# Output projection with two of its four column blocks by seven half products, the sums of weights formed by adding DMAs

## The chip, the cores and the metric

The kernel runs on one core of one Trainium2 chip. The metric is the device time of one execution in microseconds (us); lower is better. The kernel before takes 1097.7 us, the median of 3 runs (1097.32 to 1098.1).

## The reference

One layer of a hybrid decoder trunk on 512 tokens of width 2048, all in float32. With h = RMSNorm(x), the program computes

```python
z = h @ W_in                       # columns: r, k, v, two small loras | gate | pool input | pool gate
...                                # token shift, decay, rate
S_t = S_{t-1} (diag(w_t) - kk_t^T (a_t * kk_t)) + v_t^T k_t        # 16 heads of 64
y_t = S_t r_t                      # then a norm per head and a bonus
y_pool = pooled means @ w_pool * pool_scale
y_mix = concat(y_rwkv * silu(gate), y_pool * silu(pool gate))
x = x + y_mix @ W_out
x = x + sigmoid(x @ W_pg + b_pg) * (p @ W_ple)
return rms_norm(x, final_g)
```

The change is about `y_mix @ W_out`: 512 x 2048 times 2048 x 2048.

## The kernel before, in words

Every large product is made of three TensorE matmuls: each operand is split into a rounded part (hi) and a rest (lo), and `mm3` (L157) issues hi·hi, lo·hi and hi·lo into one PSUM bank. A tile of weights is 128 x 512 (256 KB). `wsplit` (L127 to L134) loads it on SyncE's (SP's) queue, casts it on ACT (`whi`, L132) and subtracts on DVE (`wlo`, L133); the weight tiles have four buffers. `split` (L136 to L139) does the same for activations (L137 on ACT, L138 on DVE).

The program runs in this order. First x is loaded, normed and transposed into `hhi`, `hlo`. Then the columns of z are produced one block after the other. Their matmuls come from a stream (`pump`) that fills TensorE between the steps of the recurrence, in the order of the program: TensorE's instructions stand in a pinned order there (`pin[0]`, `keep_in_program_order`), so a matmul that waits holds all that follow. The eight pairs of heads are prepared one after the other: `prepare_key`, `decay_and_rate`, `norm_key`, `scale_key`, `prepare`, `scores`, `invert`, `gather`, and then `recur` runs the recurrence in eight chunks of 64 tokens. Of a pair, the steps of which the prediction speaks are these:

- `decay_and_rate` casts the small weights of the loras on ACT (`us`, `uaz`, `as`: L524, L525) and multiplies by them (`pu`, `pa`); `norm_key` squares the keys into `kqh` and sums them by a matmul (`pss`). The loads of the small weights go over ACT's own DMA queue (L354).
- `invert` works on DVE, with one copy on POOL (`xw<-i`, L660).
- `recur` updates the state per chunk: a product `ps` on TensorE, then on DVE `sbd` = `ps` times a column of `pw` plus `s0p` (L807, L809), where `s0p` is the old state with its decay, formed on POOL (L816).

The output projection (`proj` with "o", L940) comes after the last recurrence. `y_mix` returns from DRAM in sixteen tiles of 128 x 512 (`load_y`, `yin`, L918) and is split into `yhi`, `ylo`. Each of four blocks of 512 columns takes 16 tiles of weights (in the order `order`), and per tile 4 groups of 128 tokens with 3 matmuls each: 192 matmuls of 512 columns a block, 768 in all. After each block DVE adds the residual (L995), ACT's queue stores the sum (`x2d`), and `turn` transposes it on TensorE (L1002) and splits it (`x2hi`, `x2lo`) for the gate's projection `acc_g`, which follows.

The tile scheduler orders the instructions of each engine; outside the pinned part they may stand in another order than the code.

Of the kernel before, what the change touches and what calls it, by code (L numbers as in the profile page):

```python
# [28 lines left out]
O_U, O_GP = O_G + DR, O_G + 2 * DR  # L29
KAPPA = math.exp(-0.5)  # L30
CK = 4


@with_exitstack
def trunk_kernel(ctx: ExitStack, tc: tile.TileContext, x, p, norm_g, w_in, mu, w0, w_up, a0, a_up,
# [84 lines left out]
    def dp(o, i):  # L120
        return dprm[:, o + i:o + i + 1]

    hhi = hp.tile([P, KT, T], F32R, name="hhi", tag="ahi")
    hlo = hp.tile([P, KT, T], F32R, name="hlo", tag="alo")


    def wsplit(src, kt, n, nm):  # L127
# [277 lines left out]
    def pool_unit(n):  # L405
        g, i = n // 4, n % 2
        win = WINDOWS[g]
        ps = psA.tile([P, T], F32, name=f"zb{n}", tag="acc")
        yield from zcols(ps, f"b{n}")
        if n % 4 < 2:  # L410
            u_ = pp.tile([P, T], F32, name=f"u{n}", tag="u")
            nc.scalar.copy(u_, ps)
            s_ = u_
            w_ = 1
            while w_ < win:
                n_ = pp.tile([P, T], F32, name=f"sw{n}_{w_}", tag="sw")
# [21 lines left out]
        nc.scalar.dma_start(out=yd[NJ + m], in_=sgp)  # L438

    phl, pn = [], []  # L440

# [314 lines left out]
    def recur(j, work, between):  # L756
# [17 lines left out]
        for ch in range(NCH):  # L774
            par, q = ch % 2, ch // 2
            pb = 64 * (1 - par)
            cur, nxt = sbd[ch % 2], sbd[(ch + 1) % 2]
            pcc = pw[:, ch, C:C + 1]
            sl = slice((ch % 4) * P, (ch % 4 + 1) * P)
            if ch % 4 == 0:  # L780
                py = psY.tile([P, T], F32, name=f"py{j}_{ch}", tag="y")
            zs = zsp[par]
            if ch > 0:
                mm(py[:, sl], ar[:, q, 2 * par:2 * par + 2, :], cur, start=ch in (1, 4), stop=True,
                                 skip_group_check=True)
# [12 lines left out]
            step()  # L798
            pump(HC2)
            if ch < NCH - 1:  # L800
                pss = psS.tile([P, T], F32, name=f"ps{j}_{ch}", tag="s")
                mm(pss[:, 0:P], bkn[:, ch, :], uv[:, ch, :], start=True, stop=True)
                for h in range(2):
                    hc = slice(64 * h, 64 * h + 64)
                    with tc.high_priority(offset=HP):
                        if ch == 0:
                            lead[0] = nc.vector.tensor_scalar(nxt[hc, hc], pss[hc, hc], pcc[hc], None, ALU.mult)  # L807
                        else:
                            lead[0] = nc.vector.scalar_tensor_tensor(nxt[hc, hc], pss[hc, hc], pcc[hc], s0p[hc, :],  # L809
                                                                     ALU.mult, ALU.add)  # L810
                s0p = rw.tile([P, C], F32, name=f"s0p{j}_{ch}", tag="s0p", bufs=2)
                pcn = pw[:, ch + 1, C:C + 1]
                if ch < NCH - 2:
                    for h in range(2):
                        hc = slice(64 * h, 64 * h + 64)
                        nc.gpsimd.tensor_scalar(s0p[hc, :], nxt[hc, hc], pcn[hc], None, ALU.mult)  # L816
# [62 lines left out]
    scale_key(0)  # L879
    prepare(0)  # L880
    pump(H3)
    scores(0)
    pump(H2)
    for _ in invert(0):
        pass
    pump(HT)
# [25 lines left out]
    yhi = ymp.tile([P, KT, T], F32R, name="yhi")  # L912
    ylo = ymp.tile([P, KT, T], F32R, name="ylo")
    AHEAD = 6

    def load_y(k):
        t_ = ymp.tile([P, T], F32, name=f"yin{k}", tag="yin", bufs=AHEAD)
        nc.scalar.dma_start(out=t_, in_=yd[k])  # L918
        split(yhi[:, k, :], ylo[:, k, :], t_)

    for k in order[:AHEAD]:
        load_y(k)
# [1 line left out]
    pin[0] = False  # L924


    x2hi = hp.tile([P, KT, T], F32R, name="x2hi", tag="ahi")
    x2lo = hp.tile([P, KT, T], F32R, name="x2lo", tag="alo")
    x2d = dram.tile([T, D], F32, name="x2d", bufs=1)

    KEEP, LATE = 8, 4
# [8 lines left out]
    def proj(w, hi_, lo_, ec, nm, ks=range(KT), tts=range(NT), keep=None, aside=None):  # L940
        acc = {tt: acc_tile(f"acc_{nm}{ec}_{tt}") for tt in tts}
        for i, k in enumerate(ks):
# [9 lines left out]
            else:  # L952
# [11 lines left out]
                keep[k] = (wh, wl)  # L964
                if i >= LATE:
                    continue
            for tt in tts if keep is None or i >= LATE else tts[:-1]:
                ts_ = slice(tt * P, (tt + 1) * P)
                first = i == (LATE if keep is not None and tt == NT - 1 else 0)
# [14 lines left out]
            nc.scalar.dma_start(out=t_, in_=pled[tt * P:(tt + 1) * P, ec * EC:(ec + 1) * EC])  # L984
            ples[ec].append(t_)

    for ec in range(D // EC):
        es = slice(ec * EC, (ec + 1) * EC)
        acc = proj(w_out, yhi, ylo, ec, "o", order)
        x2 = []  # L990
        for tt in range(NT):
            rows = slice(tt * P, (tt + 1) * P)
            t_ = pp.tile([P, EC], F32, name=f"x2_{ec}_{tt}", tag=("u", "sw")[tt // 2])
            nc.scalar.dma_start(out=t_, in_=x[rows, es])
            nc.vector.tensor_tensor(t_, acc[tt], t_, ALU.add)  # L995
            nc.scalar.dma_start(out=x2d[rows, es], in_=t_)
            x2.append(t_)
        def turn(ec=ec, x2=x2):
            for i in range(EC // P):
                pt = psM.tile([P, T], F32, name=f"px2_{ec}_{i}", tag="m")  # L1000
                for tt in range(NT):
                    nc.tensor.transpose(pt[:, tt * P:(tt + 1) * P], x2[tt][:, i * P:(i + 1) * P], ident)  # L1002
                hi = split(x2hi[:, 4 * ec + i, :], x2lo[:, 4 * ec + i, :], pt)
            return hi


        if ec < D // EC - 1:
            turn()

    sy.close()  # L1010

# [1 line left out]
    with tc.tile_pool(name="fp", bufs=2) as fp, tc.tile_pool(name="kp_", bufs=1) as kp_:  # L1013
# [92 lines left out]
        for ec in range(LAST):  # L1106
            pre = {}
            vec = vectors(ec)
            acc = proj(w_pg, x2hi, x2lo, ec, "g", aside=turn if ec == 0 else None)
# [71 lines left out]
```

## Time and profile before

| | |
|---|---|
| median of 3 runs | 1097.7 us (1097.32 to 1098.1) |
| the profiled execution | 1097.72 us |
| its span in the profile | 1095.9 us |
| TensorE (PE) busy | 1070.8 us, 98% |
| VectorE (DVE) busy | 708.2 us, 65% |
| ScalarE (ACT) busy | 448.3 us, 41% |
| GpSimd (POOL) busy | 76.9 us, 7% |
| read from and written to HBM | 118.02 MB, 18.87 MB |

The profiled execution lies at the median; 1.8 us of it are outside the span. Times in the profile are microseconds from the start of the span. Rows of the timeline give the start, the duration, the engine, the line, the operation with its operands (out<-in) and, in brackets, the idle time before it with what ended it. A busy PE is counted from overlapping records (one matmul of 512 columns is recorded with 0.39 us while the next starts 0.23 us later), so the rate is read from starts and not from durations. "ACTq" and "SPq" are the sequencers that issue DMAs.

### The profile page before, as it was taken

What the parts mean: (1) busy time and instruction counts of PE and PEld (TensorE: products, weight loads), DVE (VectorE), ACT (ScalarE), POOL (GpSimd) and SP (SyncE); (2) the same over time, 40 slices, a digit from 0 to 9 for tenths busy, and PEclk for the clock granted to TensorE, in tenths of its full rate; (3) what the DMA queues carried; (4) which work ended last, traced back from release to release, by engine and by line L of the source; (5) the groups of instructions that cost most, each with busy time, mean ns of one, the idle gap of its engine ahead of it and who ended that gap; (6) DMA issues with size and microseconds to landing.
All of it is one profiled execution on the core that took longest, in us unless ns stands there. A gap on an engine that the chain in (4) does not pass through costs nothing.

```text
span 1095.9 us, 17196 instructions
## 1 busy us (share of the span) xinstructions
PE 1070.8 (98%) x6060; PEld 877.6 (80%) x6060; DVE 708.2 (65%) x1835; ACT 448.3 (41%) x917; POOL 76.9 (7%) x180
## 2 busy tenths in 40 slices
PE   5999999999999999999999999999999999999996
PEld 4888878887788888788878788888888888888885
DVE  6687867878688679678886956454433424445366
ACT  7633535345335335353343344543222222233337
POOL 2100110110110110100101101000000000000000
PEclk9999999999999999999999999999999999999999
DMA  7433433332423333333334242775534438455534
GB/s 233 116 96 97 111 92 84 96 100 73 120 82 105 104 92 89 96 82 93 91 94 119 79 138 93 232 233 169 172 124 136 167 99 244 137 189 137 181 106 154
DMA packets 178486, 138.56 MB, mean 126 GB/s; under 512 B 34678, under 2 KB 139743, under 8 KB 178399
## 3 DMA queue, kind: packets, MB, share of 16 engines
q1 hardware_dynamic: 157694, 103.89, 32.1%
q10 hardware_dynamic: 20704, 33.56, 9.8%
q8 instruction: 48, 0.79, 0.3%
q14 instruction: 40, 0.32, 0.1%
HBM read 118.02 MB, written 18.87 MB: 125 GB/s over the span
## 4 chain that ended last, share of the span: by engine, by line
PE 86%; DVE 5%; DMA 4%; ACT 3%; issue 1%; SPq 0%; ACTq 0%; DVEq 0%
PE acc_o L157 16%; PE zb L157 14%; PE acc_g L157 14%; PE zv L157 8%; PE zk L157 7%; PE zg L157 7%; PE zr L157 7%; PE py L157 2%; PE pple L157 2%; PE pm L157 1%; PE pu L157 1%; DMA n<-nd 1%; PE pp L157 1%; DMA raw_g<-in_w_pg_dram 1%; PE ps L157 1%
## 5 line engine op out<-in xcount | busy, mean ns | idle before, releaser
L133 DVE TENSOR_TENSOR wlo_g<-raw_g,whi_g 128x512 fp32r<-128x512 f32 x84 | 57.0, 685 | 79.6 <-ACT whi_g L132 76.5
L157 PE MATMUL zb<-hhi,whi_b 128*128 128x512 f32 x256 | 107.0, 418 | 0.0
L133 DVE TENSOR_TENSOR wlo_o<-raw_o,whi_o 128x512 fp32r<-128x512 f32 x64 | 43.9, 690 | 91.4 <-ACT whi_o L132 91.4
L157 PE MATMUL zb<-hhi,wlo_b 128*128 128x512 f32 x256 | 100.5, 393 | 0.0
L157 PE MATMUL acc_o<-whi_o,ylo 128*128 128x512 f32 x256 | 100.2, 391 | 0.0
L157 PE MATMUL acc_o<-whi_o,yhi 128*128 128x512 f32 x256 | 99.9, 390 | 0.0
L157 PE MATMUL zb<-hlo,whi_b 128*128 128x512 f32 x256 | 99.9, 390 | 0.0
L157 PE MATMUL acc_o<-wlo_o,yhi 128*128 128x512 f32 x256 | 99.8, 390 | 0.0
L132 ACT CAST whi_g<-raw_g 128x512 fp32r<-128x512 f32 x84 | 51.9, 620 | 102.7 <-PE acc_g L157 55.4
L157 PE MATMUL acc_g<-whi_g,x2hi 128*128 128x512 f32 x208 | 81.3, 391 | 0.0
L157 PE MATMUL acc_g<-wlo_g,x2hi 128*128 128x512 f32 x208 | 80.9, 389 | 0.0
L157 PE MATMUL acc_g<-whi_g,x2lo 128*128 128x512 f32 x208 | 80.7, 389 | 0.0
L132 ACT CAST whi_o<-raw_o 128x512 fp32r<-128x512 f32 x64 | 39.9, 623 | 97.0 <-PE acc_o L157 96.7
L816 POOL TENSOR_SCALAR s0p<-sbd,pw 64x64 f32<-64x64 f32 x96 | 56.6, 589 | 322.8 <-DVE sbd L809 255.0
L132 ACT CAST whi_b<-raw_b 128x512 fp32r<-128x512 f32 x64 | 39.7, 621 | 86.5 <-PE zv L157 35.4
L133 DVE TENSOR_TENSOR wlo_b<-raw_b,whi_b 128x512 fp32r<-128x512 f32 x64 | 43.8, 685 | 34.2 <-ACT whi_b L132 32.9
L157 PEld LDWEIGHTS zb<-hhi,wlo_b 128*128 128x128 f32 x256 | 48.0, 188 | 11.1
L661 DVE TENSOR_TENSOR xw<-xw,tm 128x60 f32<-128x60 f32 (+24 forms) x248 | 52.1, 210 | 6.8
L157 PEld LDWEIGHTS acc_o<-wlo_o,yhi 128*128 128x128 f32 x256 | 48.1, 188 | 10.3 <-DVE wlo_o L133 0.4
L157 PEld LDWEIGHTS acc_o<-whi_o,yhi 128*128 128x128 f32 x256 | 48.1, 188 | 9.7
L157 PEld LDWEIGHTS acc_o<-whi_o,ylo 128*128 128x128 f32 x256 | 48.1, 188 | 9.8
L157 PEld LDWEIGHTS zb<-hhi,whi_b 128*128 128x128 f32 x256 | 48.2, 188 | 8.5
(285 smaller groups left out, 2550.0 us busy)
## 6 DMA issues: line engine op xcount, KB each, us to landing
raw_b<-in_w_in_dram SPq DMA_DIRECT2D x64, 256.0 KB
raw_o<-in_w_out_dram SPq DMA_DIRECT2D x64, 256.0 KB
raw_g<-in_w_pg_dram SPq DMA_DIRECT2D x64, 256.0 KB
raw_k<-in_w_in_dram SPq DMA_DIRECT2D x32, 256.0 KB
raw_r<-in_w_in_dram SPq DMA_DIRECT2D x32, 256.0 KB
raw_v<-in_w_in_dram SPq DMA_DIRECT2D x32, 256.0 KB
raw_g<-in_w_in_dram SPq DMA_DIRECT2D x32, 256.0 KB
n<-nd SPq DMA_DIRECT2D x16, 256.0 KB
```

The costliest lines, as they stand in the source:

```text
L132: nc.scalar.copy(hi, raw)
L133: nc.vector.tensor_tensor(lo, raw, hi.bitcast(F32), ALU.subtract)
L157: i = nc.tensor.matmul(*a, **k)
L661: nc.vector.tensor_tensor(xw[:, 0:n_, s + 1:32], xw[:, 0:n_, s + 1:32], tm[:, 0:n_, 0:w_], ALU.add)
L816: nc.gpsimd.tensor_scalar(s0p[hc, :], nxt[hc, hc], pcn[hc], None, ALU.mult)
```

## The change

Blocks 1 and 2 of the four column blocks are computed together by a seven-product scheme on halves: the rows of W_out are paired (tile 2q with tile 2q + 1), the tokens are cut into two halves, and in place of eight products of halves there are seven, on sums of halves. Each product takes 8 tiles of weights, and per tile 2 groups of 128 tokens with 3 matmuls: 7 x 8 x 2 x 3 = 336 matmuls for the two blocks, where there were 384. Four of the seven take sums of activations (`sab`, formed and split on DVE and ACT within block 0 and the first products), and four take sums of weights, T1 to T4 (`osum`), which lie in DRAM. The program forms these at run time. `negated` loads a pair of weight tiles (512 KB), multiplies by -1 on ACT, and stores it into the DRAM tiles, over ACT's DMA queue: 8 loads, 8 activations, 16 stores. `added` issues 20 DMAs on POOL's queue that add other weight tiles (512 KB each) to what stands there. The code calls `next(negs)` between the steps of head pair 0's preparation, and `next(adds)` once a chunk in `recur`. The tiles `hhi`, `hlo`, `x2hi`, `x2lo` become quarters, so that the sums of activations can stand where a quarter has come free. The three transposing turns come after `seven`, ahead of block 3.

The diff, cut to its core:

```diff
+    def sums_of(nm, w, c1, c2):
+        t_ = {m: dram.tile([KT // 2, P, EC], F32, name=f"sum_{nm}{m}", bufs=1) for m in (1, 2, 3, 4)}
...
+        def negated():
+            for q in range(0, KT // 2, 2):
+                for odd, c, to in ((0, c2, (1, 3, 2)), (1, c1, (4,))):
+                    raw = pp.tile([P, 2, EC], F32, name=f"neg_{nm}{q}{odd}", tag=("dh", "dl")[odd], bufs=1)
+                    nc.scalar.dma_start(out=raw, in_=pairs(w, odd, c, q))
+                    nc.scalar.activation(raw, raw, AF.Copy, scale=-1.0)
+                    for m in to:
+                        nc.scalar.dma_start(out=at(m, q), in_=raw)
+                    yield
+
+        def added():
+            for q in range(0, KT // 2, 2):
+                for m, src in ((1, pairs(w, 0, c1, q)), (3, pairs(w, 1, c2, q)), (2, pairs(w, 1, c2, q)),
+                               (2, pairs(w, 0, c1, q)), (4, at(2, q))):
+                    nc.gpsimd.dma_start(out=at(m, q), in_=src, accum_op=ALU.add)
+                    yield
...
             step()
+            next(adds, None)
...
+    osum, negs, adds = sums_of("o", w_out, 1, 2)
     need("k", 0)
+    next(negs, None)
     need("r", 0)
+    next(negs, None)
     prepare_key(0)
     decay_and_rate(0)
+    next(negs, None)
     norm_key(0)
...
+    def sab_sums(q):
...
+        nc.vector.tensor_tensor(r1, a1[:, RH], a2[:, RH], ALU.add)
+        nc.vector.tensor_tensor(r3, a1[:, LH], a1[:, RH], ALU.subtract)
+        nc.vector.tensor_tensor(r2, r1, a1[:, LH], ALU.subtract)
+        nc.vector.tensor_tensor(r4, a2[:, LH], r2, ALU.subtract)
+        sab_split(1, q)
+        sab_split(3, q)
...
+        p1, p2 = run([(rows(0, c1), own(0, 0)), (rows(1, c1), own(1, 0))], [bm, bm, bm, ba],
+                     lambda q: sab_split(2, q))
...
+        p5, p7 = run([(lambda q: osum[1][q], summed(1)), (lambda q: osum[3][q], summed(3))], [bb, bb, bb, ba],
+                     lambda q: sab_split(4, q))
+        for a in range(2):
+            a_ = tmp("a", a)
+            tt_(a_, s1[a], p5[a], sub)
+            s7 = ymp.tile([P, EC], F32, name=f"s7{a}", tag="cx", bufs=6)
+            nc.scalar.copy(s7, p7[a])
+            tt_(s1[a], s1[a], s7, add)
+            tt_(s7, s7, a_, add)
...
+        for a in range(2):
+            for ec, tt, t_ in ((c2, a, c12[a]), (c2, 2 + a, c22[a]), (c1, 2 + a, c21[a])):
+                tt_(t_, t_, res_(ec, tt), add)
+        p6, p3 = run([(lambda q: osum[2][q], summed(2)), (rows(1, c2), summed(4))], [bm, bm, bm, ba])
+        for a in range(2):
+            tt_(c12[a], p3[a], c12[a], add)
+            tt_(c12[a], p6[a], c12[a], add)
+            tt_(c22[a], p6[a], c22[a], add)
+            tt_(c21[a], p6[a], c21[a], add)
...
+        p4, = run([(lambda q: osum[4][q], own(1, 1))], [bb, bb])
...
-    for ec in range(D // EC):
+    x20 = block_o(0)
+    x21, x22 = seven(1, 2)
+    turn(0, x20)
+    turn(1, x21)
+    turn(2, x22)
+    x23 = block_o(3)
```

How the built programs stand against each other is seen on three engines. On POOL, at the start of the first recurrence, before (`x_2258` is the cleared tile of pair 1's inverse, `xw_1862` the copy of `invert`, `s0p_0` the decayed state of the first recurrence's first step):

```order
L668 MEMSET x_1142 128x512
L537 MEMSET pw_1440 128x8
L668 MEMSET x_2258 128x512
L660 COPY xw_1862<-i_116 128x256
L816 TENSOR_SCALAR s0p_0_1694<-sbd_567,pw_836 64x64 x2
L816 TENSOR_SCALAR s0p_1_1836<-sbd_566,pw_836 64x64 x2
```

The same place of the changed kernel; the first four rows are the last five of the twenty adding DMAs (`sum_o_601` to `sum_o_604` are T1 to T4), and the other fifteen stand directly ahead of them, behind `MEMSET x_2315`:

```order
L482 DMA sum_o_601<-in_w_out_dram 128x2x512
L482 DMA sum_o_603<-in_w_out_dram 128x2x512
L482 DMA sum_o_602<-in_w_out_dram 128x2x512 x2
L482 DMA sum_o_604<-sum_o_602 128x2x512
L707 COPY xw_1914<-i_116 128x256
L863 TENSOR_SCALAR s0p_0_1744<-sbd_573,pw_856 64x64 x2
L863 TENSOR_SCALAR s0p_1_1887<-sbd_572,pw_856 64x64 x2
```

All twenty stand ahead of POOL's first work for the first recurrence, none between its chunks. Each waits for the landing of the store that put the negated tile in its place, and the second add into T2 and the add into T4 wait for the landing of the add before them.

On ACT, in the preparation of head pair 0, before (`sig` and `tha` read the products `pu` and `pa`; the casts `us_561`, `uaz_570` and `as_565`, which these products need, stand 16, 15 and 7 rows above the first of these):

```order
L557 ACTIVATE kk_817<-sk_698,prm 128x512
L354 DMA ar_956<-in_a_up_dram 64x128
L137 CAST kqh_819<-kk_817 128x512
L354 DMA ar_956<-in_a_up_dram 64x128
L132 CAST whi_v_1_704<-raw_v_1_702 128x512
L132 CAST whi_v_2_710<-raw_v_2_708 128x512
L132 CAST whi_v_3_728<-raw_v_3_726 128x512
L369 ACTIVATE sr_798<-zr_701,dprm 128x512
L524 CAST us_955<-ur_952 128x128
L532 ACTIVATE sig_832<-pu_829,dprm 128x512
L547 ACTIVATE tha_844<-pa_841,dprm 128x512
L525 CAST uaz_570<-ur_952 64x128
```

The same place of the changed kernel (`neg_o_833` is the second negated pair of weight tiles):

```order
L472 DMA neg_o_833<-in_w_out_dram 128x2x512
L147 CAST whi_v_3_744<-raw_v_3_742 128x512
L384 ACTIVATE sr_814<-zr_711,dprm 128x512
L604 ACTIVATE kk_837<-sk_708,prm 128x512
L571 CAST us_567<-ur_564 128x128
L473 ACTIVATE neg_o_833<-neg_o_833 128x1024
L152 CAST kqh_839<-kk_837 128x512
L475 DMA sum_o_604<-neg_o_833 128x2x512
L572 CAST uaz_576<-ur_564 64x128
L571 CAST as_571<-ar_568 128x128
L572 CAST uaz_577<-ar_568 64x128
L472 DMA neg_o_866<-in_w_out_dram 128x2x512
```

The casts of the small weights of pair 0 and the squares of its keys (`kqh`) moved behind an activation that waits for a load of 512 KB.

On DVE, after the first block of the output projection, before (`x_0_...` are the four sums with the residual, `px` the transposed tiles):

```order
L133 TENSOR_TENSOR wlo_o_10_8528<-raw_o_10_8525,whi_o_10_8527 128x512
L995 TENSOR_TENSOR x_0_0_8441<-acc_o_0_8133,x_0_0_8441 128x512
L995 TENSOR_TENSOR x_0_1_8445<-acc_o_1_8134,x_0_1_8445 128x512
L995 TENSOR_TENSOR x_0_2_8449<-acc_o_2_8135,x_0_2_8449 128x512
L995 TENSOR_TENSOR x_0_3_8453<-acc_o_3_8136,x_0_3_8453 128x512
L138 TENSOR_TENSOR x2lo<-px_0_0_8457,x2hi 128x512
L138 TENSOR_TENSOR x2lo<-px_0_1_8464,x2hi 128x512
L138 TENSOR_TENSOR x2lo<-px_0_2_8471,x2hi 128x512
L138 TENSOR_TENSOR x2lo<-px_0_3_8478,x2hi 128x512
L133 TENSOR_TENSOR wlo_o_11_8546<-raw_o_11_8543,whi_o_11_8545 128x512
```

In the changed kernel, between the products p5, p7 and the products p6, p3 (`wlo_f` are the rests of the weight tiles of the seven products, `wlo_f_9088`, one row above, the first of p6; `a` and `s` the partial results):

```order
L148 TENSOR_TENSOR wlo_f_9100<-raw_f_9097,whi_f_9099 128x512
L1171 TENSOR_TENSOR a_9051<-s_8821,seven_8837 128x512
L1171 TENSOR_TENSOR a_9057<-s_8829,seven_8838 128x512
L148 TENSOR_TENSOR wlo_f_9112<-raw_f_9109,whi_f_9111 128x512
L1174 TENSOR_TENSOR s_8821<-s_8821,s_9053 128x512
L1174 TENSOR_TENSOR s_8829<-s_8829,s_9059 128x512
L1175 TENSOR_TENSOR s_9053<-s_9053,a_9051 128x512
L1175 TENSOR_TENSOR s_9059<-s_9059,a_9057 128x512
L1181 TENSOR_TENSOR a_9051<-a_9051,x_2_0_9063 128x512
L1181 TENSOR_TENSOR s_9053<-s_9053,x_2_2_9066 128x512
L148 TENSOR_TENSOR wlo_f_9124<-raw_f_9121,whi_f_9123 128x512
L1181 TENSOR_TENSOR s_8821<-s_8821,x_1_2_9069 128x512
```

Between the second and the fourth weight tile of the next products stand eight additions of 128 x 512 and the rest of the third tile, and two more additions follow ahead of each of the next two tiles.

More of the change, by code (lines that the diff above doesn't have):

```diff
@@ L31, with __init__, __getitem__ @@
 CK = 4
+class Quarters:
+    def __init__(self, make):
+        self.make, self.tiles = make, {}
+    def __getitem__(self, key):
+        p_, k, c = key
+        if k // 4 not in self.tiles:
+            self.tiles[k // 4] = self.make(k // 4)
+        return self.tiles[k // 4][p_, k % 4, c]
 @with_exitstack
@@ L121, in dp, with quarters @@
         return dprm[:, o + i:o + i + 1]
-    hhi = hp.tile([P, KT, T], F32R, name="hhi", tag="ahi")
-    hlo = hp.tile([P, KT, T], F32R, name="hlo", tag="alo")
+    def quarters(nm, part):
+        return Quarters(lambda c: hp.tile([P, 4, T], F32R, name=f"{nm}{c}", tag=f"{part}{c}"))
+    hhi, hlo = quarters("hhi", "h"), quarters("hlo", "l")
     def wsplit(src, kt, n, nm):
@@ L882, in trunk_kernel @@
     scores(0)
+    next(negs, None)
     pump(H2)
+    for _ in negs:
+        pass
     for _ in invert(0):
@@ L919, in load_y @@
         split(yhi[:, k, :], ylo[:, k, :], t_)
+        yin[k] = t_
     for k in order[:AHEAD]:
@@ L924, in trunk_kernel @@
     pin[0] = False
-    x2hi = hp.tile([P, KT, T], F32R, name="x2hi", tag="ahi")
-    x2lo = hp.tile([P, KT, T], F32R, name="x2lo", tag="alo")
+    x2hi, x2lo = quarters("x2hi", "h"), quarters("x2lo", "l")
     x2d = dram.tile([T, D], F32, name="x2d", bufs=1)
@@ L985, in recall, with residual, keep_x2, turn @@
             ples[ec].append(t_)
-    for ec in range(D // EC):
-        es = slice(ec * EC, (ec + 1) * EC)
+    def residual(ec, tt, pool, **kw):
+        t_ = pool.tile([P, EC], F32, name=f"x2_{ec}_{tt}", **kw)
+        nc.scalar.dma_start(out=t_, in_=x[tt * P:(tt + 1) * P, ec * EC:(ec + 1) * EC])
+        return t_
+    def keep_x2(ec, tt, t_):
+        nc.scalar.dma_start(out=x2d[tt * P:(tt + 1) * P, ec * EC:(ec + 1) * EC], in_=t_)
+    def turn(ec, x2):
+        for i in range(EC // P):
+            pt = psM.tile([P, T], F32, name=f"px2_{ec}_{i}", tag="m")
+            for tt in range(NT):
+                nc.tensor.transpose(pt[:, tt * P:(tt + 1) * P], x2[tt][:, i * P:(i + 1) * P], ident)
+            hi = split(x2hi[:, 4 * ec + i, :], x2lo[:, 4 * ec + i, :], pt)
+        return hi
+    def block_o(ec):
         acc = proj(w_out, yhi, ylo, ec, "o", order)
@@ L991, in trunk_kernel @@
         for tt in range(NT):
-            rows = slice(tt * P, (tt + 1) * P)
-            t_ = pp.tile([P, EC], F32, name=f"x2_{ec}_{tt}", tag=("u", "sw")[tt // 2])
-            nc.scalar.dma_start(out=t_, in_=x[rows, es])
+            t_ = residual(ec, tt, pp, tag=("u", "sw")[tt // 2])
             nc.vector.tensor_tensor(t_, acc[tt], t_, ALU.add)
-            nc.scalar.dma_start(out=x2d[rows, es], in_=t_)
+            keep_x2(ec, tt, t_)
             x2.append(t_)
[L998 to L1004, printed above, removed]
@@ L1108, in trunk_kernel @@
             vec = vectors(ec)
-            acc = proj(w_pg, x2hi, x2lo, ec, "g", aside=turn if ec == 0 else None)
+            acc = proj(w_pg, x2hi, x2lo, ec, "g", aside=(lambda: turn(3, x23)) if ec == 0 else None)
             ple = ples.pop(ec)
```

93 lines of the change are left out of this document (91 added, 2 removed).

## The prediction

> **What bounds the kernel now.** I read the page first: the busy line, the queues, and the chain of work that ended last.
>
> ```profile
> span 1095.9 us, 17196 instructions
> ...
> PE 1070.8 (98%) x6060; PEld 877.6 (80%) x6060; DVE 708.2 (65%) x1835; ACT 448.3 (41%) x917; POOL 76.9 (7%) x180
> ...
> q1 hardware_dynamic: 157694, 103.89, 32.1%
> q10 hardware_dynamic: 20704, 33.56, 9.8%
> ...
> PE 86%; DVE 5%; DMA 4%; ACT 3%; issue 1%; SPq 0%; ACTq 0%; DVEq 0%
> ```
>
> TensorE is busy in all but 25 us of the span and makes 86% of the chain. Fewer matmuls pay only if nothing else makes it wait, and every new wait of TensorE counts in full. So I asked next, by stretches, where the other engines and the DMA have room (columns: window, then length and busy time of PE, PEld, DVE, ACT, POOL, then the granted clock, the DMA share and GB/s).
>
> ```profile
> 27.00:55.00 28.00, 28.00 (x163) 24.70 (x162) 18.25 (x45) 17.82 (x38) 2.93 (x11) 1.00 0.42 114
> 55.00:82.00 27.00, 27.00 (x143) 22.32 (x142) 22.18 (x33) 10.50 (x20) 0.00 (x0) 1.00 0.35 97
> 82.00:110.00 28.00, 28.00 (x125) 23.17 (x124) 20.25 (x76) 8.83 (x15) 0.00 (x0) 1.00 0.33 96
> 110.00:137.00 27.00, 27.00 (x233) 21.94 (x232) 22.24 (x37) 14.19 (x30) 3.33 (x3) 1.00 0.42 112
> 137.00:700.00 563.00, 559.50 (x3560) 455.40 (x3558) 430.93 (x1291) 237.49 (x520) 64.23 (x112) 1.00 0.35 100
> ...
> 727.00:780.00 53.00, 53.00 (x242) 43.57 (x241) 27.49 (x43) 20.73 (x36) 0.00 (x0) 1.00 0.56 183
> 780.00:830.00 50.00, 50.00 (x230) 41.37 (x229) 17.25 (x26) 13.16 (x22) 0.00 (x0) 1.00 0.47 156
> ```
>
> The first four rows are the stretch in which the sums of weights are now formed. TensorE has no idle time there, and the DMA engines are already a third to two fifths busy. The fifth is the recurrence. The last two are blocks 0 and 1 of the output projection: full TensorE again, DVE half and a third busy.
>
> **What is removed: 48 matmuls.** The pitch of the projection's matmuls, first and last of thirteen consecutive starts:
>
> ```profile
> 769.62 0.39 PE L157 MATMUL acc_o<-whi_o,ylo 128*128 128x512 f32 x1
> ...
> 772.34 0.39 PE L157 MATMUL acc_o<-whi_o,ylo 128*128 128x512 f32 x1
> ```
>
> 2.72 us over 12 steps is 0.2267 us each. Blocks 1 and 2 go from 384 to 336, so 48 x 0.2267 = **-10.9 us**, on the path.
>
> **What is added late, on DVE.** The rows for one operation, the eviction after block 0, and ACT's rhythm:
>
> ```profile
> L133 DVE TENSOR_TENSOR wlo_o<-raw_o,whi_o 128x512 fp32r<-128x512 f32 x64 | 43.9, 690 | 91.4 <-ACT whi_o L132 91.4
> L132 ACT CAST whi_o<-raw_o 128x512 fp32r<-128x512 f32 x64 | 39.9, 623 | 97.0 <-PE acc_o L157 96.7
> L133 DVE TENSOR_TENSOR wlo_wp<-raw_wp,whi_wp 128x256 fp32r<-128x256 f32 x8 | 3.3, 410 | 1.4 <-ACT whi_wp L132 1.4
> L1002 PE MATMUL px<-ident,x 128*128 128x128 f32 x64 | 9.1, 277 | 0.7 <-DVE x2lo L138 0.7
> 771.32 2.48 DVE L995 TENSOR_TENSOR x<-acc_o,x 128x512 f32<-128x512 f32 x4
> 788.30 0.62 ACT L132 CAST whi_o<-raw_o 128x512 fp32r<-128x512 f32 x1 [2.05 <-PE acc_o L157]
> 791.02 0.62 ACT L132 CAST whi_o<-raw_o 128x512 fp32r<-128x512 f32 x1 [2.10 <-PE acc_o L157]
> ```
>
> A weight tile now feeds 12 matmuls (2.72 us, the distance of the two casts). In the seven products it feeds 6, so 1.36 us; one cast (0.62) and one subtraction (0.69) still fit into that. But the four buffers now cover half the time, and DVE works in order. The order of DVE between p5, p7 and p6, p3 shows the pile-up. At the end of p7 two tiles are ready (2.72 us of TensorE). DVE does two subtractions, the third tile (ready at 3 x 0.69 = 2.07), then six additions and the fourth tile (10 x 0.69 = 6.9). TensorE has run dry at 3 x 1.36 = 4.08: 2.8 us of waiting. Ahead of each of the next two tiles stand two additions (3 x 0.69 = 2.07 per tile against 1.36): 0.7 us twice. With some 0.3 for handing over that is 4.5. Between p3 and p4 eight additions and a tile (9 x 0.69 = 6.2) stand against three ready tiles (4.08), and the first addition can start 0.7 earlier, with p3's first half: 1.4 us. At the end of p4 the last two subtractions and the first transposes have little ahead of them that covers them: 2 x 0.69 and a store's issue, about 1.8. Before, the turns cost TensorE 0.7 us in all (the row of `px`). So **+7**, between 0 (the scheduler's ready tiles are more than I count) and 10.9. In block 0 the sums of activations add 48 operations of 128 x 256: 48 x 0.41 = 19.7 on DVE, 27.5 + 19.7 = 47.2 of 53: tight, and I cost it at nothing; if that cover is gone, it is a few us here.
>
> Net of the late part: -10.9 + 7 = **-4 us** (0 to -10.9).
>
> **What is added early, on ACT.** Rows of ACT, then of TensorE, in head pair 0's preparation:
>
> ```profile
> 39.86 0.30 ACT L524 CAST us<-ur 128x128 fp32r<-128x128 f32 x1
> 40.06 0.29 ACT L525 CAST uaz<-ur 64x128 fp32r<-64x128 f32 x1
> ...
> 51.99 0.62 ACT L137 CAST kqh<-kk 128x512 fp32r<-128x512 f32 x1
> ...
> 54.95 0.62 ACT L132 CAST whi_v<-raw_v 128x512 fp32r<-128x512 f32 x1 [1.76 <-PE zr L157]
> ```
> ```profile
> 58.38 0.39 PE L157 MATMUL pu<-uhh,us 128*128 128x512 f32 x1
> 58.60 0.39 PE L157 MATMUL pu<-lal,uaz 128*128 128x512 f32 x1
> ...
> 59.28 0.39 PE L157 MATMUL pss<-kqh,blk 128*128 128x512 f32 x1
> ```
>
> The casts were done 7 to 18 us before `pu` and `pss` wanted them. In the changed order `kqh`, `uaz` and `as` stand behind the activation on `neg_o_833`, whose load is issued only after the third cast of `whi_v`, at 54.95 + 0.62 = 55.6. How long such a load takes is bounded from below by a load of 256 KB with others around it on the same queue:
>
> ```profile
> 718.03 0.82 ACTq L918 DMA_DIRECT2D yin<-yd  x2
> ...
> 723.14 0.62 ACT L137 CAST yhi<-yin 128x512 fp32r<-128x512 f32 x1 [3.48 <-DMA yin<-yd]
> ```
>
> 5.1 us, so it lands at 60.7. From above: three stores of 512 KB stand ahead in its queue, and four such DMAs at the rate below and with 0.35 of the engines taken need 4 x 1.68 / 0.65 = 10.3, so 65.9. Then the activation (1024 columns, about two casts, 1.2), `kqh` 0.62, `uaz` 0.3: `pu`'s second matmul at 62.8 to 68.0 in place of 58.6. TensorE waits 4 to 9.5; I take 6. Later `kph` stands behind a second such load:
>
> ```profile
> 74.27 0.62 ACT L137 CAST kph<-kp 128x512 fp32r<-128x512 f32 x1 [1.01 <-DVE kp L601]
> ```
> ```profile
> 77.45 0.50 PE L157 MATMUL pbo<-kph,blk 128*128 128x512 f32 x1
> ```
>
> Its cover is 77.45 - 74.89 = 2.6, so a load of 5.1 costs 2.5 (0 to 5). Together **+8.5** by the time the recurrence starts, if nothing worse follows.
>
> **What is added early, on POOL and the DMA engines.** Where POOL stands, and when its first result is wanted:
>
> ```profile
> 38.76 0.52 POOL L668 MEMSET x<- 128x512 f32 x1
> 125.38 2.44 POOL L660 COPY xw<-i 128x256 f32<-128x256 f32 x1 [86.10 <-PE px L157]
> 129.68 0.98 POOL L816 TENSOR_SCALAR s0p<-sbd,pw 64x64 f32<-64x64 f32 x2 [1.86 <-DVE sbd L807]
> ```
> ```profile
> 143.04 0.60 DVE L809 SCALAR_TENSOR_TENSOR sbd<-ps,pw,s0p 64x64 f32<-64x64 f32 x2 [2.35 <-PE ps L157]
> ```
>
> POOL idles from 39.3 to 125.4, which looks like free room. But all twenty adds stand ahead of `xw` and `s0p`, and each waits for landings. Until the last is issued, `s0p` isn't formed; then `sbd` at 143.0 waits, DVE behind it, the next `ps` and `py` behind that, and in TensorE's pinned order everything else. So the deadline for the last add is about 143, and the first negated load goes out at about 40: 103 us. The queues' rows above price a DMA: q10 moved 33.56 MB in 9.8% of 1095.9 = 107.4 us of all sixteen engines, 312 GB/s, so 1.68 us for 0.524 MB. The 8 loads and 16 stores of `negated` take 24 x 1.68 = 40.3. The weights that the streams load anyway take 15 x 0.42 + 27 x 0.35 + 28 x 0.33 + 27 x 0.42 + 6 x 0.35 = 38.4. No row shows an adding DMA. As a copy, the lower end, twenty take 33.6. At double, the upper end, 67.1: two reads and a write that shut each other out. I take one and a half, 50.3, three streams where a copy has two. The Trainium skill ("DMA: Bandwidth & Descriptors", section "Rules for kernel authors") says that an accumulating DMA reads its destination and writes it later; no run here shows that yet, and by it the third stream would be there.
>
> Sum: 40.3 + 38.4 + 50.3 = 129 against 103: 26 over; the last add need only be issued, not landed, which gives back its 2.5: **+24** (+8 at the copy's price, +40 at the double, by the same sum). The waits of ACT lie inside it, since they hold up the same recurrence that then waits for POOL anyway. Behind the start, nothing brings the time back: TensorE is busy 559.5 of 563 us from 137 to 700.
>
> Sum against the profiled 1097.72, which lies at the median: +24 - 4 = **1118 us**.
>
> **The rivals.** *Adds at a copy's price.* POOL is then no later than ACT's waits: +8.5 - 4 gives 1102. For it: nothing in this trace shows an adding DMA slower than a copy. Against it: the adds of a group wait for one another. *Faster.* The other side, one mechanism: the negated load is back early. It decides whether the load behind `whi_v` lands by about 57, 1.5 us after its issue; then the casts are in time, the adds trickle into POOL's 86 idle us, and the late part stays: 1097.7 - 4 to - 10.9 with 1 to 2 of handing over, 1088 to 1095. Against it: the 5.1 us row. For it: my late +7 rests on counted rows alone. If early waits and late gain cancel, the time stays within 0.2%, about 2.2 us, which is what a measurement of this kernel can tell. *Adds far slower.* At the double price or above: +40 - 4 gives 1134, and another half of the adds' time (20 us) on top gives 1154. For it stands how long POOL's copy takes on average, over its eight instances:
>
> ```profile
> L660 POOL COPY xw<-i 128x256 f32<-128x256 f32 x8 | 8.0, 1001 | 210.4 <-PE px L157 189.8 <-DMA raw_r<-in_w_in_dram 20.5
> ```
>
> The mean is 1.0 us, and the one at 125.38 took 2.44, beside a DVE busy 22 of 27 us. So POOL can be slower beside a busy DVE, and if writing the adds' orders is held up likewise, they crawl. The Trainium skill ("SBUF — State Buffer", section "SBUF: two separate sides") warns of just that: a DMA from GpSimd's queue waits while DVE holds the shared port; no run here shows it for a DMA.
>
> **How the numbers follow.** Forecast (POOL lets the recurrence start about 24 us late) 0.40; adds at a copy's price 0.17; adds far slower 0.15; cancelling 0.07; faster 0.21. Slower is 0.40 + 0.17 + 0.15 = 0.72, within 0.2% 0.07, faster 0.21. The range 1091 to 1146 leaves out the lower third of the faster case and the upper half of the slowest, some 0.15. The forecast's own range, by the prices of its terms, is 1102 to 1134.
>
> **What would show it.** Right: POOL's first `s0p` starts well after 143 and ends its wait on a DMA; TensorE has its longest idle time there, released by DVE's `sbd`; a smaller gap of 4 to 9 us at `pu` released by ACT; 4 to 5 us of waiting for `wlo_f` after p7; from the last recurrence to the gate 4 us less than before. Wrong: `s0p` in time and TensorE without gaps up to 143; or the late part longer than before; or gaps in block 0 released by the sums of activations.

## The result, and the profile after

The changed kernel takes 1145.95 us, the median of 4 runs (1140.46 to 1148.07; a fifth on record, not in the median, took 1151.88), against 1097.9 (1097.32 to 1098.48): the ratio is 1.0442, with a 95% interval of 1.0397 to 1.0488. It is 48 us slower, where 20 were forecast; the time lies at the upper edge of the range 1091 to 1146. The profiled execution is the fastest of the four, 1140.46 us with a span of 1138.7, which is 42.8 us over the span before.

The page after, with the lines that answer to those of before: busy time, granted clock and DMA share in 40 slices, the queues (packets, MB, share of the sixteen engines), the chain.

```profile
span 1138.7 us, 17447 instructions
...
PE 1071.9 (94%) x6012; PEld 874.9 (77%) x6012; DVE 756.3 (66%) x1941; ACT 484.3 (43%) x985; POOL 97.5 (9%) x200
...
PEclk9988799999999999999999999999999999999998
DMA  7599994233333243333333334376566636554534
...
q1 hardware_dynamic: 161150, 110.19, 33.1%
q10 hardware_dynamic: 27232, 46.15, 12.2%
q0 software_dynamic: 5440, 10.49, 5.4%
...
PE 71%; DMA 12%; DVE 10%; ACT 3%; issue 2%; SPq 1%; ACTq 0%; DVEq 0%
```

TensorE's share of the chain fell by 15 points, and DMA's rose from 4% to 12%. The slices show where: from the third to the sixth the DMA engines are at nine tenths. The new row q0 is POOL's adding DMAs: 5.4% of 1138.7 = 61.5 us of all sixteen engines for twenty adds, 3.07 us each. By stretches (columns as in the prediction):

```profile
27.00:55.00 28.00, 28.00 (x162) 24.72 (x163) 17.32 (x42) 16.70 (x33) 3.99 (x12) 1.00 0.52 153
55.00:82.00 27.00, 18.79 (x75) 14.72 (x74) 15.00 (x21) 11.81 (x20) 5.95 (x6) 0.87 1.04 278
82.00:110.00 28.00, 21.09 (x103) 16.78 (x102) 9.46 (x16) 6.87 (x12) 6.64 (x7) 0.82 1.10 259
110.00:137.00 27.00, 13.19 (x52) 10.43 (x52) 12.11 (x48) 3.56 (x6) 3.19 (x4) 0.75 0.96 232
137.00:165.00 28.00, 24.33 (x156) 18.99 (x156) 18.29 (x42) 15.19 (x30) 4.95 (x5) 0.94 1.00 232
```

TensorE, without a gap here before, idles in all rows but the first, and the DMA share there is 0.96 to 1.10. (A share above 1 means that the recorded times of packets overlap; what is called engine time below is the sum of such times.) The granted clock falls to 0.75. From 27 us to POOL's first `s0p` TensorE does 605 recorded matmuls in both kernels: before in 102.7 us without a gap, here in 147.0, of which it is busy 112.6. So 34.4 us are idle time and 9.9 are slower work (busy time times the missing clock, row by row, would give 11), together the 44.3 by which the recurrence is late. POOL's timeline shows its first `s0p` at 174.0, against 129.7.

```profile
53.95 1.34 POOL L482 DMA_DIRECT2D sum_o<-in_w_out_dram  x1 [14.50 <-DMA sum_o<-neg_o]
...
168.02 1.14 POOL L482 DMA_DIRECT2D sum_o<-sum_o  x1 [5.98 <-DMA sum_o<-in_w_out_dram]
168.71 0.85 POOL L707 COPY xw<-i 128x256 f32<-128x256 f32 x1
173.98 0.98 POOL L863 TENSOR_SCALAR s0p<-sbd,pw 64x64 f32<-64x64 f32 x2 [4.42 <-DVE sbd L854]
```

The last row already speaks against the mechanism that I forecast: with its adds done, POOL waited 4.4 us for DVE's `sbd`. What was late is seen in the chain of waits between 38 and 180 us (start, duration, what). Its longest pieces, beside stretches of matmuls, are transfers:

```profile
55.14 10.30 DMA neg_o<-in_w_out_dram
...
84.72 17.70 DMA raw_r<-in_w_in_dram
...
103.31 5.63 DMA nd<-mt
109.10 14.43 DMA n<-nd
...
143.90 5.78 DMA xd<-xw
149.76 5.74 DMA ur<-in_w_up_dram
```

An exchange over DRAM (`n<-nd`), a tile of weights (`raw_r`) and a negated load take 10 to 18 us. The same exchange of pair 0 before and after, as DVE's first step of `invert` waits for it:

```profile
89.28 0.19 DVE L657 TENSOR_TENSOR tm<-i,n 128x31 f32<-128x31 f32 x1 [3.83 <-DMA n<-nd]
```
```profile
123.55 0.19 DVE L704 TENSOR_TENSOR tm<-i,n 128x31 f32<-128x31 f32 x1 [18.07 <-DMA n<-nd]
```

Its first DMA was issued at 82.8 before and at 109.1 here, so it took 6.5 us before and 14.4 here. TensorE's waits name the engine that handed them on (us in all, times, longest):

```profile
PE zr L172 <- DVE sg L389: 13.8, 1, 13.8
PE pu L172 <- ACT uaz L572: 9.1, 2, 6.6
PE pbo L172 <- ACT kph L152: 6.9, 1, 6.9
```

For the stages behind, the rows of the first `acc_o` and `acc_g` matmuls (first and last start), before and after:

```profile
L157 PE MATMUL acc_o<-whi_o,yhi x256: 388/389/474, 728.8 to 908.2; 128*128 128x512 f32 x128
L157 PE MATMUL acc_g<-whi_g,x2hi x208: 388/389/476, 908.9 to 1061.4; 128*128 128x512 f32 x104
```
```profile
L172 PE MATMUL acc_o<-whi_o,yhi x128: 389/389/482, 777.0 to 952.0; 128*128 128x512 f32 x128
L172 PE MATMUL acc_g<-whi_g,x2hi x208: 388/389/478, 952.7 to 1104.1; 128*128 128x512 f32 x104
```

So the sum of this execution, 5 us faster than the median, is: start of the recurrence +44.3; recurrence +3.9 (728.8 to 777.0 is 48.2 later); output projection 175.7 against 180.1, so -4.4; gate and end -1.0. That makes +42.8.

### The profile page after: what moved, and what is told of

It reads as the page before. It is cut to its first block, busy times and chain, and to the rows that moved or that the text cites. A ratio compares the mean times of both kernels' runs of the same rounds, so it can differ in the third digit from the quotient of the medians.

```text
span 1138.7 us, 17447 instructions
## 1 busy us (share of the span) xinstructions
PE 1071.9 (94%) x6012; PEld 874.9 (77%) x6012; DVE 756.3 (66%) x1941; ACT 484.3 (43%) x985; POOL 97.5 (9%) x200
## 3 DMA queue, kind: packets, MB, share of 16 engines
q0 software_dynamic: 5440, 10.49, 5.4%
## 4 chain that ended last, share of the span: by engine, by line
PE 71%; DMA 12%; DVE 10%; ACT 3%; issue 2%; SPq 1%; ACTq 0%; DVEq 0%
PE acc_g L172 15%; PE zb L172 12%; PE zv L172 7%; PE seven L172 6%; PE zr L172 5%; PE zg L172 5%; PE zk L172 5%; DMA n<-nd 5%; PE acc_o L172 4%; PE py L172 2%; PE pple L172 2%; DMA raw_r<-in_w_in_dram 2%; PE pu L172 1%; DMA yin<-yd 1%; DVE tm L704 1%
## 5 line engine op out<-in xcount | busy, mean ns | idle before, releaser
L172 PE MATMUL zr<-hhi,whi_r 128*128 128x512 f32 x128 | 54.3, 424 | 13.8 <-DVE sg L389 13.8
L147 ACT CAST whi_f<-raw_f 128x512 fp32r<-128x512 f32 x56 | 34.3, 622 | 49.1 <-DMA raw_f<-in_w_out_dram 16.8
L704 DVE TENSOR_TENSOR tm<-xw,n 128x60 f32<-128x60 f32 (+10 forms) x240 | 50.7, 211 | 6.5
L172 PEld LDWEIGHTS zb<-hhi,whi_b 128*128 128x128 f32 x256 | 48.2, 188 | 8.5
L172 PEld LDWEIGHTS zb<-hlo,whi_b 128*128 128x128 f32 x256 | 48.3, 189 | 8.0
L148 DVE TENSOR_TENSOR wlo_f<-raw_f,whi_f 128x512 fp32r<-128x512 f32 x56 | 37.5, 692 | 24.9 <-ACT whi_f L147 24.5
L172 PE MATMUL zv<-hhi,whi_v 128*128 128x512 f32 x128 | 53.7, 420 | 0.0
L172 PE MATMUL zg<-hhi,whi_g 128*128 128x512 f32 x128 | 53.6, 419 | 0.0
L172 PE MATMUL zk<-hhi,whi_k 128*128 128x512 f32 x128 | 53.1, 415 | 0.0
## 6 DMA issues: line engine op xcount, KB each, us to landing
sum_o<-in_w_out_dram POOLq DMA_DIRECT2D x16, 512.0 KB, 10.3
```

Of the source, the lines that this page charges most:

```text
L147: nc.scalar.copy(hi, raw)
L148: nc.vector.tensor_tensor(lo, raw, hi.bitcast(F32), ALU.subtract)
L172: i = nc.tensor.matmul(*a, **k)
L704: nc.vector.tensor_tensor(tm[:, 0:n_, 0:w_], xin[:, 0:n_, s:s + 1].to_broadcast([P, n_, w_]), nb[s // 16][:, s % 16:s % 16 + 1, s + 1:32]. ...
```

## The experiments

The theories: A, mine, that the adds stand ahead of `s0p` on POOL and hold the recurrence; B, that the adds and the negated tiles fill the DMA engines while head pair 0's preparation depends on one small transfer after another; C, that an add costs by slowing the stream of weights wherever it lies; D, that it is the number of the adds and their chain of landings. Ratios are to the kernel before, measured beside each group, whose median was 1097.1 to 1097.3 us; costs in us are read from the ratios.

**Without sums.** The generators are empty; the seven products read plain rows of W_out (not shown), so blocks 1 and 2 are not the projection.

```diff
-    osum, negs, adds = sums_of("o", w_out, 1, 2)
+    osum, negs, adds = None, iter(()), iter(())
```

> The sums of weights are left out: neither the negated tiles nor the adds are made, and the seven products read plain rows of W_out in their place (so the output's blocks 1 and 2 are not the projection). Everything else of the change stays. This measures the late part alone. Both theories of the early part (POOL's order; full DMA engines) expect no early delay at all: pair 0's first s0p at 129.7 us as before. For the late part, the profile of the changed kernel shows the stretch from the first matmul of the projection to the gate's first at 175.7 us against 180.1 before, and the tail 1.0 us shorter: so 1092.5 us, 1091 to 1094. The full worth of the 48 matmuls would be 1087.

Measured 1096.11 us, ratio 0.9988 (0.9974 to 1.0001). The early delay is gone, as all theories have it. The late part alone is worth 1 us in the medians (1091 to 1094 us was expected), and the interval reaches no gain at all. The profiled execution, 1093.49 us, is at the fast end of the runs (1091.61 to 1099.56); its stage of the output projection takes 176.3 us, 180.1 before. Its TensorE timeline and DVE's, where p5, p7 end:

```profile
825.79 0.50 PE L172 MATMUL seven<-wlo_f,sh 128*128 128x512 f32 x1 [2.85 <-DVE wlo_f L148]
830.33 0.50 PE L172 MATMUL seven<-wlo_f,sh 128*128 128x512 f32 x1 [0.86 <-DVE wlo_f L148]
```
```profile
818.49 1.28 DVE L1171 TENSOR_TENSOR a<-s,seven 128x512 f32<-128x512 f32 x2
819.68 0.69 DVE L148 TENSOR_TENSOR wlo_f<-raw_f,whi_f 128x512 fp32r<-128x512 f32 x1
820.29 1.28 DVE L1174 TENSOR_TENSOR s<-s,s 128x512 f32<-128x512 f32 x2
821.49 1.28 DVE L1175 TENSOR_TENSOR s<-s,a 128x512 f32<-128x512 f32 x2
823.76 0.69 DVE L1181 TENSOR_TENSOR a<-a,x 128x512 f32<-128x512 f32 x1 [0.98 <-DMA x<-in_x_dram]
824.45 0.69 DVE L1181 TENSOR_TENSOR s<-s,x 128x512 f32<-128x512 f32 x1
825.06 0.68 DVE L148 TENSOR_TENSOR wlo_f<-raw_f,whi_f 128x512 fp32r<-128x512 f32 x1
```

Between two weight tiles DVE does six additions, and TensorE waits 2.85 us for the second: the pile-up that the order showed. But 0.98 us of DVE's time there is a wait for a load of `x`, which the order did not show.

**Without adds.** The sums stay the negated tiles.

```diff
     osum, negs, adds = sums_of("o", w_out, 1, 2)
+    adds = iter(())
```

> The twenty adds are left out (the sums stay the negated tiles), loads, negations and stores stay. Theory A (the adds stand ahead of pair 0's s0p on POOL and hold the recurrence) and theory B (the adds fill the DMA engines, 3.1 us each, and everything that comes by DMA is late) both expect most of the delay gone. What stays is the waits of ACT for the negated loads: TensorE waited 6.6 + 1.6 us at pu and 6.9 us at pbo in the changed kernel. With the stores still ahead of the load in its queue I expect 6 to 15 us of that to stay: 1092.5 + 6 to 15 = 1098 to 1108 us. If the early cost were nothing but the adds, 1092.5.

Measured 1108.3 us, ratio 1.0112 (1.0099 to 1.0125). The eight loads and sixteen stores cost 1.24% or 14 us over the kernel without sums; the twenty adds, up to the 1.0442 of the changed kernel, 3.3% or 36 us. DVE's wait for pair 0's exchange `n<-nd` is 6.8 us here, against 18.1 with the adds.

**Adds as copies.** The DMAs move the same bytes, but add nothing.

```diff
-                    nc.gpsimd.dma_start(out=at(m, q), in_=src, accum_op=ALU.add)
+                    nc.gpsimd.dma_start(out=at(m, q), in_=src)
```

> The twenty DMAs on POOL's queue are plain copies into the same places, with the same waits and order (so the sums are not formed). Theory B: the price of the adding is what counts; the queue's share falls from 61.5 us of the sixteen engines to about 34 (1.7 us for each), and the time falls by most of those 28 us, to 1118 to 1126. If the price is that of DMAs from POOL's queue as such, the share stays near 60 us and the time near 1146. Theory A expects the last of the twenty to be issued earlier only as far as the landings that they wait for come earlier, so between the two.

Measured 1127.96 us, ratio 1.0285 (1.0269 to 1.0301). The queue's row:

```profile
q0 software_dynamic: 2880, 10.49, 2.8%
```

2.8% of its span, 1123.9, is 31.5 us, 1.57 each: adding costs 1.95 times the copy. The time fell by 1.57% or 17 us, to 2 us above the expected 1118 to 1126. So the adding itself is about half of what the twenty DMAs cost.

**s0p on DVE.** Nothing that the first recurrence needs stands behind the adds.

```diff
-                        nc.gpsimd.tensor_scalar(s0p[hc, :], nxt[hc, hc], pcn[hc], None, ALU.mult)
+                        (nc.vector if j == 0 else nc.gpsimd).tensor_scalar(s0p[hc, :], nxt[hc, hc], pcn[hc], None, ALU.mult)
```

(and the same for the copy `xw` of pair 1).

> The first recurrence's s0p and the copy xw for pair 1 run on DVE, so that nothing that the first recurrence needs stands behind the adds on POOL; adds, negations and all DMAs stay as they are. Theory A: the recurrence no longer waits for POOL, so up to 24 us come back: 1120 to 1130. Theory B: in the changed kernel POOL's s0p waited 4.4 us for DVE's sbd after its last add, so POOL wasn't last; the DMA engines stay full to about 168 us, and the time stays at 1140 to 1150.

Measured 1147.5 us, ratio 1.0461 (1.0445 to 1.0478): nothing came back. Theory A falls. Its first `sbd` and the `s0p` behind it, on DVE:

```profile
182.27 0.60 DVE L854 TENSOR_SCALAR sbd<-ps,pw 64x64 f32<-64x64 f32 x2 [0.45 <-PE ps L172]
182.90 0.53 DVE L863 TENSOR_SCALAR s0p<-sbd,pw 64x64 f32<-64x64 f32 x2
```

Its first `s0p` comes 9 us later than in the changed kernel's profile, though it follows `sbd` at once; why later isn't settled. The share of the DMA engines from 55 to 175 us is 0.92 to 1.07 here too.

**A quarter of each add.** Same order on every engine, same waits, but each add moves 128 of 512 columns (the sources are narrowed likewise, not shown), so three quarters of the sums are not formed.

```diff
-                    nc.gpsimd.dma_start(out=at(m, q), in_=src, accum_op=ALU.add)
+                    nc.gpsimd.dma_start(out=at(m, q)[:, :, 0:P], in_=src, accum_op=ALU.add)
```

> The changed kernel, with its order on every engine and its waits, but each of the twenty adds moves only 128 of its 512 columns (so three quarters of the sums stay the negated tiles). If the cost of the adds is their bytes on the DMA engines (theory B: 39 us for all of them), about a quarter or less of it stays: 1108.3 + 0 to 10 = 1108 to 1118 us. If it is their number, their fixed time and the chain of landings that each waits for (rival D), most of it stays: 1130 to 1147.

Measured 1119.55 us, ratio 1.0201 (1.0188 to 1.0214), 1.5 us above the range for B and far from D.

```profile
q0 software_dynamic: 5440, 2.62, 2.1%
```

The packets are as many, the bytes a quarter, and the engines' time 2.1% of 1118.1 = 23.5 us. With the engines' time in q0 at 0, 23.5, 31.5 and 61.5 us, the ratio rises over that without adds by 0.9, 1.7 and 3.3% (the last from the changed kernel itself): 10, 19 and 36 us, 0.4 to 0.6 us for each us of the engines. D falls: with all twenty and all their waits, most of the cost went. Whether the engines themselves are full or the memory behind them, these runs don't separate.

**Adds behind s0p.** One add goes out per chunk of the first three recurrences; the negated tiles stay in the preparation.

```diff
-            next(adds, None)
+            with tc.issue_after(plead[0].ins):
+                next(adds, None)
```

(`plead` is POOL's last `s0p`.)

> The adds are tied behind POOL's s0p, so that one goes out per chunk of the first three recurrences; the negated loads and stores stay in the preparation of pair 0. Theory B (what counts is how much DMA work falls into the preparation of pair 0, where each wait for a load or an exchange is on the path): the adds cost nothing or little where they are now, since one of 3.1 us per chunk of 6 to 7 us beside weights that take 0.35 of the engines still fits. So the time without adds (1108.3 us) plus 0 to 4: 1108 to 1112. Rival C (an add costs by slowing the stream of weights wherever it lies): the 39 us that the adds cost stay for the most part, 1130 to 1147.

Measured 1113.74 us, ratio 1.0151 (1.0128 to 1.0174): 0.4% or 4 us over the kernel without adds, instead of 36. The adds take no less of the engines (6.0% of 1113.2 = 67 us):

```profile
q0 software_dynamic: 5440, 10.49, 6.0%
```

But there the DMA share, adds included, is 0.62 to 0.77, and TensorE hardly idles:

```profile
137.00:200.00 63.00, 62.31 (x386) 50.40 (x379) 44.78 (x148) 23.12 (x53) 19.41 (x23) 1.00 0.77 160
200.00:300.00 100.00, 98.69 (x684) 80.00 (x684) 82.26 (x222) 46.01 (x100) 22.09 (x27) 1.00 0.62 138
```

Exchanges of the later pairs run beside the adds there: DVE waits 2.4, 2.2 and 4.3 us for those of pairs 1 to 3, against 2.3, 0.5 and 3.1 before. C falls, B stands: not the adds' work costs, but their work in that stretch.

**All sums in the recurrences.** The negated tiles go out in the recurrences of pairs 3 and 6, the adds in those of pairs 4 to 7.

```diff
+    LOADS = {(3, 0): 0, (3, 1): 1, (3, 3): 2, (3, 4): 3, (3, 6): 4, (3, 7): 5, (6, 0): 6, (6, 1): 7}
+    STORES = {(3, 2): 0, (3, 3): 1, (3, 5): 2, (3, 6): 3, (3, 8): 4, (3, 9): 5, (6, 2): 6, (6, 3): 7}
```

> The whole change, with nothing of the sums in the preparation of pair 0: the eight negated loads go out in the recurrences of pairs 3 and 6, each activation two chunks behind its load, the adds in those of pairs 4 to 7, five each behind POOL's s0p. Theory B: the early cost goes, and what is left is the kernel without sums (1096.1 us) plus 0 to 4 for the DMA work that now lies in the recurrence: 1096 to 1100. Rival C: 1130 or more.

Measured 1105.1 us, ratio 1.0062 (1.0045 to 1.0078): the delay before the first recurrence is gone, but 0.74% or 8 us are left over the kernel without sums, where I expected up to 4. POOL's `s0p` shows the place: the last of pair 3 and the first of pair 4, before and here.

```profile
396.25 1.04 POOL L816 TENSOR_SCALAR s0p<-sbd,pw 64x64 f32<-64x64 f32 x2 [4.58 <-DVE sbd L809]
...
430.91 1.78 POOL L816 TENSOR_SCALAR s0p<-sbd,pw 64x64 f32<-64x64 f32 x2 [4.65 <-DVE sbd L807]
```
```profile
395.57 1.05 POOL L865 TENSOR_SCALAR s0p<-sbd,pw 64x64 f32<-64x64 f32 x2 [5.83 <-DVE sbd L858]
...
437.81 1.78 POOL L865 TENSOR_SCALAR s0p<-sbd,pw 64x64 f32<-64x64 f32 x2 [3.98 <-DVE sbd L856]
```

From 0.7 us ahead to 6.9 behind, right behind the six tiles that pair 3's recurrence was given; that these are the cause is tested below.

**Additions spread, no sums.** Again plain rows of W_out are read. The additions behind p5, p7 are done between the weight tiles of p6, p3, and those behind p6, p3 between the tiles of p4.

```diff
-        p6, p3 = run([(lambda q: osum[2][q], summed(2)), (rows(1, c2), summed(4))], [bm, bm, bm, ba])
+        p6, p3 = run([(rows(0, c2), summed(2)), (rows(1, c2), summed(4))], [bm, bm, bm, ba],
+                     lambda q: some(post, 2))
```

> The sums of weights are left out as in the kernel without sums (plain rows of W_out are read, so blocks 1 and 2 are not the projection); what changes is only when DVE does the additions between the products: those behind p5, p7 are spread over p6, p3, two per pair of weight tiles, and those behind p6, p3 over p4, one per tile. If the pile-up on DVE is what eats the late gain (my 4.5 and 1.4 us; the profile without sums shows TensorE 4.2 us waiting for wlo_f), 3 to 6 us come back against 1096.1: 1090 to 1093. If the late loss is elsewhere (the clock, the turns, block 0), it stays at 1095 to 1097.

Measured 1094.14 us, ratio 0.9962 (0.9949 to 0.9976), against 0.9988 (0.9974 to 1.0001) with the pile-up: 0.26% or 3 us, with intervals that just touch; the time is above the expected 1090 to 1093. The profile does not show where the gain is: the stage takes 176.6 us, against 176.3 with the pile-up (the profiled execution, 1096.24 us, is the slowest of its runs). TensorE's waits for `wlo_f` fell, but its other waits in this stage rose:

```profile
PE acc_o L172 <- DVE wlo_o L148: 1.5, 1, 1.5
PE px L1092 <- DVE x2lo L153: 1.4, 1, 1.4
PE seven L172 <- DVE wlo_f L148: 1.3, 4, 0.7
```

The first is in block 0, under the sums of activations.

**Both edits,** the last two diffs together, with the real sums.

> The whole change, with the sums formed in the recurrences of pairs 3 to 7 and the additions between the products spread: the two edits before this one together. Theory B and the pile-up: 1090 to 1097, below the kernel before. Rival C: 1125 or more. If the pile-up isn't the late loss: the same as the version with the sums in the recurrence alone.

Measured 1105.13 us, ratio 1.0063 (1.0044 to 1.0082): no better than with the sums in the recurrences alone. 1090 to 1097 was expected. The 3 us of the spread additions don't show, and why is open.

**Negated tiles spread.** Of the six tiles in pair 3's recurrence, two are loaded behind it and stored behind the next gather, and two others go one chunk later (not shown); the additions stay spread.

```diff
+        if j == 3:
+            with tc.issue_after(alead[0].ins):
+                neg_load(4)
+                neg_load(5)
```

> The whole change with the additions between the products spread, as in the version before it with the sums in the recurrence (1105.1 us); that one lost 7.6 us between the last s0p of pair 3 (0.7 us ahead of the kernel before) and the first of pair 4 (6.9 us behind), where six negated tiles lay packed and ACT waited for their loads. Now four negated tiles go out in pair 3's recurrence, two are loaded behind it and stored behind the next gather, two stay in pair 6. If that packing was the loss, 4 to 7 us come back: 1098 to 1101 us, still not below the kernel before (1097.2). If it is the DMA work as such (40 us for the negated tiles and 62 for the adds, wherever they lie), it stays at 1103 to 1107.

Measured 1100.64 us, ratio 1.0031 (1.0016 to 1.0046): 0.32% or 3.5 us came back against 1.0063 (4.5 in the medians; 4 to 7 were expected), with intervals that just touch. The first `s0p` of pair 4 is at 433.4 us, 2.5 behind the kernel before in place of 6.9, so the packing was part of the loss. It is the best whole version, and still slower than the kernel before. At best, with sums that cost nothing, the change is worth the 0.4% that the version without them and with the additions spread has shown.

## Why the prediction was wrong, point by point

**48 matmuls for 10.9 us, 7 of them given back on DVE:** right in this profile, -4.4 us for the stage against -4. TensorE's busy time in the stage fell by 8.7 us (180.1 to 171.4), and 4.3 us of idle time came in, of which 2.8 are waits for `wlo_f`. The pile-up is shown, but the 2.85 us where the order gave 2.8 are partly luck: they hold the wait for `x`. In repeated runs the net gain without sums is only 1 us in the medians, and 3 with the additions spread; what takes the rest of 10.9 isn't settled, apart from the 1 to 2 us waits above.

**ACT behind the negated load:** the wait was right, its size by luck. The load was issued at 55.14 and took 10.3 us, at the upper bound; `pu` waited 6.6 for `uaz` at once, inside my 4 to 9.5, and `pbo` 6.9, above my 0 to 5. But three adds were beside that load, which I had not counted there: without adds it took 6.6 us, and the two waits were 2.9 and 1.0. All of the negating still costs 14 us without the adds, where I had +8.5 from these two waits.

**The adds' price:** this term was mis-sized. "As a copy, the lower end, twenty take 33.6. At double, the upper end, 67.1 ... I take one and a half, 50.3." The copies took 31.5 and the adds 61.5, 1.95 times. At the double price my sum read +40 for the start of the recurrence, and the profile has +44.3; that is luck, as the next point shows. The Trainium skill's rule ("DMA: Bandwidth & Descriptors", section "Rules for kernel authors"), that an accumulating DMA reads its destination and writes it later, fits the doubled time; but the rows of q0 have 10.49 MB for adds and copies alike, so no run shows that read itself.

**POOL's order as the gate:** this step failed: "Until the last is issued, s0p isn't formed; then sbd at 143.0 waits". My +24 meant that the last add is issued at about 143 + 24 = 167, and `sbd` follows. The last add was issued at 168.0, but that `sbd` came at 187.3:

```profile
187.34 0.60 DVE L856 SCALAR_TENSOR_TENSOR sbd<-ps,pw,s0p 64x64 f32<-64x64 f32 x2 [2.35 <-PE ps L172]
```

And my sign for POOL as the gate, that its first `s0p` ends its wait on a DMA, did not come; it waited for DVE. With `s0p` off POOL the time stayed at 1147.5. The engines were as full as the sum had it. The queues of the changed kernel between 40 and 175 us:

```profile
q0 software_dynamic: 5440, 10.49, 45.9%
q10 hardware_dynamic: 7713, 13.46, 27.5%
q1 hardware_dynamic: 19329, 8.76, 25.1%
```

That is 62 + 37 + 34 = 133 us of work in 135. But they hold the recurrence earlier, by the loads and exchanges of the preparation. I had counted the DMA work and then let only POOL wait for it; what waited were ACT for the negated load (10.3 us, 6.6 without the adds), DVE for the exchange (18.1, 6.8 without the adds) and, behind them, TensorE.

**Not counted:** the clock, 9.9 us of slower work on TensorE at 0.75 to 0.94, and 3.9 us in the recurrence, whose cause is open.

**The rivals.** "Adds far slower", 1134 to 1154, is where the time came out; I gave it 0.15. Its doubled price was right, but it had POOL as the gate too, so that the time fell into it is luck. Its picture of POOL held up beside a busy DVE was not seen: the issues on POOL took 1.14 us each from the fourth on, as in the row at 168.02, in stretches with DVE busy 34 to 65%. The trap in the Trainium skill ("SBUF — State Buffer", section "SBUF: two separate sides") is tied to DVE operations of one kind, those in a 2-port mode; these rows don't show it, and no run tested it.

## What to carry to other kernels

Background transfers are to be priced by engine time, and put where the DMA engines have room: the same twenty adds cost 36 us in a stretch that was filled to 1.0, where one small transfer after another is waited for, and 4 us where the share stayed below 0.8, although exchanges ran there too. When a sum says that a shared resource is full, ask who waits for it first, not who stands last in the queue. And check what the program's order makes of a call: `next(adds)` once a chunk became twenty adds ahead of the first chunk.

## What the runs showed of the hardware

An adding DMA from DRAM to DRAM cost 3.07 us of the sixteen engines for 512 KB, a copy on the same queue 1.57. The twenty adds went out in 5440 packets, the twenty copies in 2880 for the same bytes; at a quarter of the bytes the adds kept their 5440 packets and 38% of the time (23.5 of 61.5 us). TensorE's granted clock fell to 0.87, 0.82 and 0.75 in stretches where it was busy 70%, 75% and 49% of the time. Behind a wait of 6.9 us that ended at 95.0, matmuls of 512 columns started 0.43 us apart until 101.4, and 0.23 us apart from there on.
